# A hybrid decoder layer on one core: a reordered start, head halves in alternation, and two small moves at the ends of the MLP

## The chip, the cores and the metric

The kernel runs on one core of a Trainium2 chip. The metric is the device time of one execution in microseconds (us), median over runs. Engines are called as in the profile: PE is TensorE (PEld its weight loads), DVE VectorE, ACT ScalarE, POOL GpSimd, SP the engine that issues most DMAs. "L92" is line 92 of the kernel before.

## The reference

One decoder layer, batch 1, 256 tokens, width 2048, all in float32:

```python
h = rmsnorm(x, norm_mix_pre)
xr, yr, q, k, v, g_rnn, g_attn = split(h @ w_in)
y_rnn = rg_lru(causal_conv(xr)) * gelu(yr)
y_att = sliding_window_sink_attention(rope(q), rope(k), v, sinks)   # 32 heads, 4 key/value heads of 64
mix = sigmoid(g_rnn) * (y_rnn @ w_rnn_proj) + sigmoid(g_attn) * (y_att @ w_attn_proj)
x = x + rmsnorm(mix @ w_out, norm_mix_post)
h = rmsnorm(x, norm_mlp_pre)
u = square(relu(h @ w_mlp_up))                                       # 8192 wide
x = x + rmsnorm(u @ w_mlp_down, norm_mlp_post)
```

## The kernel before

Every large product is made from split operands: a float32 value is stored as a rounded high part and the low part that is left, and a product is the sum of high x high, high x low and low x high, three matmul passes. Weights stream from HBM in halves of 128 x 1024 (512 KB). For each, ACT writes the high part (`whi`, L91) and DVE subtracts it for the low part (`wlo`, L92). There are six buffers of each, and `Stream.ahead` keeps the splitting six halves ahead of the products.

The program is written in Python order. A scheduler then orders each engine's instructions by priority (the order of writing) and by when its own model takes the inputs to be ready. `pin` (`keep_in_program_order`) fixes an instruction behind the one written before it on its engine, `issue_after` fixes an order of issue without a wait, and `high_priority(n)` moves a block ahead by n places.

The start: the 256 tokens are two blocks of 128 (`tb`). Their x is loaded in quarters of 512 columns, ACT squares each quarter (`square`), `rms` gives the factor, DVE multiplies by factor and gain (`scale`, L349), PE transposes (`turn`, L355), and ACT and DVE store the high and low part of the transposed quarter (`part`, L361 and L362) in `hT`. The gain is spread to 128 partitions by PE: a tile of zeros with the gain in row 0, multiplied by ones (`gain_b`, L339). Between these steps stand the first k/v products (`kv_step`, which calls `b_step`, L251 to L255) for the first weight halves. The order is written out by hand, and nearly all of it is pinned. `warm` (L333) are matmuls without use for the result, issued while x is on its way.

Attention runs as a generator for each group g of key heads, one piece of it at a time between other matmuls (`pump`). The scores (`sc`, L527) take 64 rows of PE: heads of `par` 0 lie on partitions 0 to 63, those of `par` 1 on 64 to 127. The PSUM pool `psm` has two banks, which scores, transposes (`pt`) and outputs (`po`) share. For the first token block (w = 128) one bank holds four heads; for the second (w = 256) it holds two.

The MLP: `a_pair` makes a pair of 128-wide blocks of the up projection in one of two PSUM pairs (`ps`); ACT copies one half out and DVE adds the other (L240, L241). `down` begins by taking both pairs for itself (`s`), with four other banks. It forms seven of its sixteen steps by a seven-product scheme, whose sums `early` picks up; the other products and `finish` follow. At the very end (f = 1, n = 1) `finish` adds the last sums (L1033), squares them (L1037), multiplies by the gain (L1038), takes the norm and writes the output. The first half of the columns (`acc`) is multiplied by the gain in `early` (L1026).

Of the kernel before, what the change touches and what calls it, by code (L numbers as in the profile page):

```python
# [16 lines left out]
F32 = mybir.dt.float32  # L17
# [3 lines left out]
ALU = mybir.AluOpType  # L21
AX = mybir.AxisListType

P = 128
D = 2048
S = 256
TB = 2
# [24 lines left out]
class Stream:  # L52
# [35 lines left out]
    def two_parts(self, src, j):  # L88
        hi = self.pool.tile([P, 1024], F32R, tag="whi", bufs=WHALF, name=f"whi{j}")
        lo = self.pool.tile([P, 1024], F32R, tag="wlo", bufs=WHALF, name=f"wlo{j}")  # L90
        self.pin(self.nc.scalar.copy(hi, src))  # L91
        self.pin(self.nc.vector.tensor_tensor(lo, src, hi.bitcast(F32), ALU.subtract))  # L92
        return hi, lo

    def split_sums(self, j):
# [54 lines left out]
def layer(tc, x, pos_t, pos_row, inv_freq, vecs, sinks, gains, w_kv, w_q, w_xy, w_rg, w_g, w_rp, w_ap, w_out,  # L150
# [52 lines left out]
    def bank(pool, name):  # L203
        return pool.tile([P, 512], F32, tag=pool.name, name=name)
# [19 lines left out]
    def a_pair(acts, out):  # L224


        ps = pair("ps")
        for f in range(2):
            both = ps[:, f].rearrange("p a b -> p (a b)")
            for half in range(2):  # L230
                hi, lo = ws.half()
                act = [acts[kt // 4][:, kt % 4] for kt in range(half * 8, half * 8 + 8)]
                for k, a in enumerate(act):
                    mm(both, hi[:, k * P : k * P + P], a.rearrange("p a b -> p (a b)"),  # L234
                       start=half == 0 and k == 0, stop=False)
# [4 lines left out]
        nc.scalar.copy(out, ps[:, :, 1, :])  # L240
        nc.vector.tensor_tensor(out, ps[:, :, 0, :], out, ALU.add)  # L241

    def b_step(banks, acts, kt, hi, lo, last, tbs=(0, 1)):

# [47 lines left out]

    x_nat = [flat(unit(f"x{tb}", F32)) for tb in range(TB)]
    x_v = x.rearrange("(t p) d -> t p d", p=P)
    gain = flat(unit("gain", F32))
    nc.vector.memset(gain, 0.0)
    nc.scalar.dma_start(gain[0:1, :], gains[0:1])

    def quarter(q):
        return slice(q * 512, q * 512 + 512)  # L300

    for q in range(4):
        last = nc.sync.dma_start(x_nat[0][:, quarter(q)], x_v[0][:, quarter(q)])
    with tc.issue_after(last.ins):
        ws.load_to(2)
        for q in range(4):
            last = nc.sync.dma_start(x_nat[1][:, quarter(q)], x_v[1][:, quarter(q)])
# [4 lines left out]
    eps = const.tile([P, 1], F32, name="eps")  # L312
    nc.vector.memset(eps, EPS)
    st = const.tile([P, 32], F32, name="st")
    sq = const.tile([P, 4, TB, 4], F32, name="sqs")
    ones = const.tile([P, P], F32, name="ones")
    nc.vector.memset(ones, 1.0)
    make_identity(nc, ident)
    nc.scalar.activation(st[:, 31:32], eps, AF.Sqrt)

# [23 lines left out]
    def square(tb, q):  # L344
        pin(nc.scalar.activation(t2("j"), x_nat[tb][:, quarter(q)], AF.Square, accum_out=sq[:, 0, tb, q : q + 1]))

    def scale(tb, q, r):
        c = quarter(q)
        pin(nc.vector.scalar_tensor_tensor(x_nat[tb][:, c], x_nat[tb][:, c], r, gain_b[q], ALU.mult, ALU.mult))  # L349
# [13 lines left out]

    kv = [[bank(psb, f"kv{tb}")] for tb in range(TB)]

    def kv_step(j, hi, lo, tbs):
        for i in range(2):
            c = slice(i * 512, i * 512 + 512)
            b_step(kv, hT, 2 * j + i, hi[:, c], lo[:, c], 2 * j + i == KT - 1, tbs)

    for q in range(4):
        square(0, q)
    r = rms(0, 0)
    scale(0, 0, r)
    scale(0, 1, r)
    turn(0, 0)
    ws.split_to(1)
    square(1, 0)
    part(0, 0)
    turn(0, 1)  # L380
    square(1, 1)
    scale(0, 2, r)
    ws.split_to(2)
    held = [ws.half(False) for j in range(2)]
    square(1, 2)
    part(0, 1)
    turn(0, 2)
    square(1, 3)
    scale(0, 3, r)
    kv_step(0, *held[0], (0,))  # L390
    part(0, 2)
    turn(0, 3)
    r = rms(1, 0)
    scale(1, 0, r)
    part(0, 3)
    kv_step(1, *held[1], (0,))
    turn(1, 0)
    scale(1, 1, r)
    part(1, 0)
    turn(1, 1)  # L400
    ws.split_to(3)
    scale(1, 2, r)
    part(1, 1)
    turn(1, 2)
    kv_step(0, *held[0], (1,))
    ws.split_to(4)
    scale(1, 3, r)
    part(1, 2)
    turn(1, 3)
    part(1, 3)  # L410
    kv_step(1, *held[1], (1,))
    for j in range(2, 8):
        if j == 4:
            ws.pin = lambda i: i
        kv_step(j, *ws.half(), (0, 1))

    pos_i = pa.tile([P, TB], I32, name="pos_i")
    nc.sync.dma_start(pos_i, pos_t)
    ifr = pa.tile([P, 32], F32, name="ifr")
    nc.sync.dma_start(ifr, inv_freq.partition_broadcast(P))  # L420
    sink = pa.tile([P, NH], F32, name="sink")
    nc.sync.dma_start(sink, sinks.partition_broadcast(P))
    vec = pa.tile([P, 8, KT], F32, name="vec")
    nc.sync.dma_start(vec, vecs.rearrange("p (a b) -> p a b", a=8))


    mask1 = pa.tile([P, S], F32, name="mask1")
# [68 lines left out]
    def attention(g, banks):  # L496
# [11 lines left out]
        for tb in range(TB):  # L508
# [9 lines left out]
            stat = pa.tile([P, 4, 8], F32, tag="stat", bufs=3, name="stat")  # L518
            sk = sink[:, 8 * g : 8 * g + 8]
            tiles = []  # L520
            for par in range(2):
                r0 = par * HD
                for j in range(4 // per):
                    ps = bank(psm, "sc")
                    for i in range(per):
                        h = j * per + i
                        mm(ps[:, i * w : i * w + w], qT[r0 : r0 + HD, h, tb * P : tb * P + P],  # L527
                           kT[r0 : r0 + HD, g, 0:w], start=True, stop=True)
# [25 lines left out]
            for par in range(2):  # L554
                for kb in range(nk):
                    ps = bank(psm, "pt")
                    for h in range(4):
                        s3, at = tiles[par * (4 // per) + h // per]
# [413 lines left out]
    for f in range(2):  # L972
# [39 lines left out]
        def early(ready):  # L1012
# [6 lines left out]
            for i in range(2):  # L1019
                g = wpool.tile([P, 1024], F32, tag="wraw", bufs=WRAW, name=f"g3{i}")  # L1020
                nc.sync.dma_start(g, gains[3][i * 1024 : i * 1024 + 1024].partition_broadcast(P))
                g3.append(g)
            for tb in range(TB):
                for i in range(2):
                    c = quarter(i)
                    nc.vector.tensor_tensor(acc[tb][:, c], acc[tb][:, c], g3[0][:, c], ALU.mult)  # L1026

        def finish(name, b, t):
            tb, i = name
# [8 lines left out]
            nc.vector.tensor_tensor(t, a, g3[1][:, quarter(i)], ALU.mult)  # L1038
# [89 lines left out]
```

## Time and profile before

| | |
|---|---|
| median of 3 runs | 1552.69 us (1552.5 to 1554.2) |
| the profiled execution | 1553.58 us, span 1551.8 us |
| mean granted PE clock | 0.993 |
| PE busy | 1525.7 us (98%) |
| DVE, ACT, POOL busy | 1117.5, 843.9, 1.7 us |
| read from HBM | 288.60 MB, 190 GB/s over the span |

The span runs from the first to the last instruction; the profiled execution's own time is 1.78 us longer. In a row of the timeline stand the start and the length of a run of equal instructions, the engine (a q behind it: its sequencer), the line, what is written from what, the shapes, the count, and in brackets the idle time of the engine before it with what ended it. A row of the waits gives who waited for whom, the total, the number of times and the longest. A row of the windows gives the stretch, its length, then busy time and count of PE, PEld, DVE, ACT and POOL, the granted PE clock, the DMA engines' share and GB/s. Matmuls overlap their neighbours in these rows, so the pace of PE is read from start to start.

### The profile page before, as it was taken

The numbers are of one execution on the slowest core, as the hardware profiler recorded it, in microseconds if no ns is written. First come the engines' busy times: TensorE is split into PE (matmuls) and PEld (weight loads), VectorE is DVE, ScalarE is ACT, GpSimd is POOL, SyncE is SP. The second block draws the span as 40 slices with busy tenths as digits, with TensorE's granted clock in tenths as the row PEclk, the third lists the DMA queues.
The fourth block names the chain that finished last, engine by engine and source line by source line (L and its number), as shares of the span: only waits on it lengthen the run. The fifth ranks groups of instructions, "written<-read, shape, count | busy, mean of one in ns | idle before, by whom it ended". The sixth has DMA issues, their size and how long they took to land.

```text
span 1551.8 us, 20974 instructions
## 1 busy us (share of the span) xinstructions
PE 1525.7 (98%) x8042; PEld 1295.5 (83%) x8042; DVE 1117.5 (72%) x1364; ACT 843.9 (54%) x1156; POOL 1.7 (0%) x9
## 2 busy tenths in 40 slices
PE   8999999999999999999999999999999999999997
PEld 6887777888888888888787888888888888888885
DVE  6666666866859877555655866688886666788997
ACT  5555545646647766444344655555454555555553
POOL 0000000000000000000000000000000000000000
PEclk9999999999999999999999999999999999999999
DMA  6554354354655465555663855556666655566664
GB/s 246 188 169 148 115 173 147 124 191 149 229 188 177 158 213 198 190 184 190 250 221 98 278 190 189 187 175 213 218 203 218 221 187 189 188 242 232 203 216 138
DMA packets 82902, 296.26 MB, mean 191 GB/s; under 512 B 9585, under 2 KB 9841, under 8 KB 81777
## 3 DMA queue, kind: packets, MB, share of 16 engines
q1 hardware_dynamic: 79344, 285.48, 55.7%
q10 hardware_dynamic: 3458, 9.45, 1.6%
q8 instruction: 63, 1.03, 0.3%
q14 instruction: 37, 0.30, 0.1%
HBM read 288.60 MB, written 6.29 MB: 190 GB/s over the span
## 4 chain that ended last, share of the span: by engine, by line
PE 87%; DVE 5%; ACT 3%; DMA 3%; issue 2%; SPq 0%; DVEq 0%; ACTq 0%
PE ps L234 36%; PE ps L237 18%; PE dQ L908 7%; PE s L908 4%; PE dP L908 3%; DVE wlo L92 2%; PE dCs L908 2%; DMA wraw<-in_w_dn 2%; PE o L251 2%; PE o L255 2%; PE o L253 2%; PE q L251 2%; PE q L253 2%; PE q L255 2%; PE sc L527 1%
## 5 line engine op out<-in xcount | busy, mean ns | idle before, releaser
L92 DVE TENSOR_TENSOR wlo<-wraw,whi 128x1024 fp32r<-128x1024 f32 x528 | 639.8, 1221 | 322.4 <-ACT whi L91 317.0
L91 ACT CAST whi<-wraw 128x1024 fp32r<-128x1024 f32 x528 | 549.0, 1049 | 585.9 <-PE ps L234 271.5
L234 PE MATMUL ps<-hT,whi 128*128 128x512 f32 x1024 | 260.5, 394 | 0.0
L234 PE MATMUL ps<-h2T,whi 128*128 128x512 f32 x1024 | 258.2, 394 | 0.5 <-DVE h2T L280 0.5
L234 PEld LDWEIGHTS ps<-hT,whi 128*128 128x128 f32 x1024 | 183.8, 189 | 36.5 <-issue 3.5
L234 PEld LDWEIGHTS ps<-h2T,whi 128*128 128x128 f32 x1024 | 185.3, 190 | 34.2 <-DVE h2T L280 0.9
L237 PEld LDWEIGHTS ps<-hT,wlo 128*128 128x128 f32 x1024 | 140.1, 190 | 11.7 <-issue 2.0
L237 PEld LDWEIGHTS ps<-h2T,wlo 128*128 128x128 f32 x1024 | 140.0, 191 | 10.1
L237 PE MATMUL ps<-hT,wlo 128*128 128x256 f32 x1024 | 145.3, 283 | 0.0
L237 PE MATMUL ps<-h2T,wlo 128*128 128x256 f32 x1024 | 143.0, 283 | 0.0
L908 PE MATMUL dQ<-whi,uT 128*128 128x512 f32 x288 | 106.5, 389 | 0.0
L234 PE MATMUL ps<-yrnn,whi 128*128 128x512 f32 x256 | 64.4, 393 | 0.7 <-DVE yrnn L700 0.7
L234 PE MATMUL ps<-yatt,whi 128*128 128x512 f32 x256 | 64.1, 392 | 0.0
L908 PEld LDWEIGHTS dQ<-whi,uT 128*128 128x128 f32 x288 | 54.1, 188 | 11.2
L908 PE MATMUL dQ<-wlo,uT 128*128 128x512 f32 x144 | 56.1, 390 | 1.6 <-DVE wlo L92 1.6
L111 DVE TENSOR_TENSOR tlo<-t,thi 128x1536 fp32r<-128x1536 f32 x28 | 49.2, 1757 | 10.1 <-ACT thi L110 10.1
L908 PE MATMUL dP<-whi,uT 128*128 128x512 f32 x144 | 53.8, 389 | 0.0
L908 PE MATMUL dCs<-whi,uT 128*128 128x512 f32 x144 | 53.7, 389 | 0.0
L234 PEld LDWEIGHTS ps<-yrnn,whi 128*128 128x128 f32 x256 | 46.0, 189 | 9.3 <-DVE yrnn L700 1.1
L234 PEld LDWEIGHTS ps<-yatt,whi 128*128 128x128 f32 x256 | 46.0, 189 | 8.2
L251 PE MATMUL q<-whi,hT 128*128 128x512 f32 x128 | 51.1, 399 | 0.0
L253 PE MATMUL q<-wlo,hT 128*128 128x512 f32 x128 | 50.2, 392 | 0.0
(251 smaller groups left out, 2068.6 us busy)
## 6 DMA issues: line engine op xcount, KB each, us to landing
wraw<-in_w_up SPq DMA_DIRECT2D x128, 512.0 KB, 4.6
wraw<-in_w_dn SPq DMA_DIRECT2D x128, 512.0 KB, 4.5
wraw<-in_w_g SPq DMA_DIRECT2D x64, 512.0 KB, 4.4
wraw<-in_w_xy SPq DMA_DIRECT2D x64, 512.0 KB, 3.9
wraw<-in_w_q SPq DMA_DIRECT2D x32, 512.0 KB, 4.3
wraw<-in_w_ap SPq DMA_DIRECT2D x32, 512.0 KB, 3.8
wraw<-in_w_rp SPq DMA_DIRECT2D x32, 512.0 KB, 4.6
wraw<-in_w_out SPq DMA_DIRECT2D x32, 512.0 KB, 4.8
```

What stands on the lines that cost most here:

```text
L91: self.pin(self.nc.scalar.copy(hi, src))
L92: self.pin(self.nc.vector.tensor_tensor(lo, src, hi.bitcast(F32), ALU.subtract))
L111: v.tensor_tensor(lo, t, hi.bitcast(F32), ALU.subtract)
L234: mm(both, hi[:, k * P : k * P + P], a.rearrange("p a b -> p (a b)"), start=half == 0 and k == 0, stop=False)
L237: mm(ps[:, f, 1, :], lo[:, k * P : k * P + P], a[:, 0, :], start=False, stop=half == 1 and k == 7)
L251: mm(banks[tb][n], a[:, 0, t], hi[:, n * 512 : n * 512 + 512], start=first, stop=False)
L253: mm(banks[tb][n], a[:, 0, t], lo[:, n * 512 : n * 512 + 512], start=False, stop=False)
L255: mm(banks[tb][n], a[:, 1, t], hi[:, n * 512 : n * 512 + 512], start=False, stop=last)
L527: mm(ps[:, i * w : i * w + w], qT[r0 : r0 + HD, h, tb * P : tb * P + P], kT[r0 : r0 + HD, g, 0:w], start=True, stop=True)
L908: mm(b, a[x], w[y], start=not begun and i == 0, stop=tail and i == 2)
```

## The change

Four things are changed.

*The start.* `eps` and `ones` are set first; the gain's tile is cleared in quarters, three by DVE and one by POOL. x is loaded in two halves a block. The odd quarters are squared by DVE (`square_v`). Three scalings of the first block come ahead of the first weight splits. The low parts of the first four weight halves are subtracted on POOL (`ws.low = nc.gpsimd`). The k/v products are split into those with the high and those with the low weights (`kv_part`) and placed anew, and the halves from the third to the sixth are split at written places (`split`). Four small loads (`pos_i`, `ifr`, `sink`, `vec`) are queued behind x.

*Attention.* The loops over `par` and over the heads change places, with two banks taken at once.

*The last up pair.* For p = 15, in both f, the copy and the addition at the end of `a_pair` have a higher priority (300).

*The finish.* The four multiplications of `acc` by the gain go from `early` to `finish`, two for each token block.

```diff
@@ Stream @@
+        self.low = nc.vector
...
-        self.pin(self.nc.vector.tensor_tensor(lo, src, hi.bitcast(F32), ALU.subtract))
+        self.pin(self.low.tensor_tensor(lo, src, hi.bitcast(F32), ALU.subtract))
@@ a_pair @@
-        nc.scalar.copy(out, ps[:, :, 1, :])
-        nc.vector.tensor_tensor(out, ps[:, :, 0, :], out, ALU.add)
+        with tc.high_priority(prio) if prio else ExitStack():
+            nc.scalar.copy(out, ps[:, :, 1, :])
+            nc.vector.tensor_tensor(out, ps[:, :, 0, :], out, ALU.add)
@@ the loads @@
-    nc.vector.memset(gain, 0.0)
-    nc.scalar.dma_start(gain[0:1, :], gains[0:1])
...
+    for q in range(4):
+        (nc.gpsimd if q == 3 else nc.vector).memset(gain[:, quarter(q)], 0.0)
+    nc.scalar.dma_start(gain[0:1, :], gains[0:1])
+
+    def load_x(tb):
+        for c in (slice(0, 1024), slice(1024, 2048)):
+            last = nc.sync.dma_start(x_nat[tb][:, c], x_v[tb][:, c])
+        return last
@@ the first norm @@
+    def square_v(tb, q):
+        c = quarter(q)
+        pin(nc.vector.scalar_tensor_tensor(t2("j"), x_nat[tb][:, c], 1.0, x_nat[tb][:, c], ALU.mult, ALU.mult,
+                                           accum_out=sq[:, 0, tb, q : q + 1]))
...
+    def kv_part(j, tb, low):
+        for i in range(2):
+            kt = 2 * j + i
+            c = slice(i * 512, i * 512 + 512)
+            a, t = hT[kt // 4][:, kt % 4], slice(tb * P, tb * P + P)
+            hi, lo = held[j]
+            if low:
+                mm(kv[tb][0], a[:, 0, t], lo[:, c], start=False, stop=kt == KT - 1)
+            else:
+                mm(kv[tb][0], a[:, 0, t], hi[:, c], start=kt == 0, stop=False)
+                mm(kv[tb][0], a[:, 1, t], hi[:, c], start=False, stop=False)
...
+    square(0, 0)
+    square_v(0, 1)
+    square(0, 2)
+    square_v(0, 3)
+    r = rms(0, 0)
+    ws.low = nc.gpsimd
+    scale(0, 0, r)
+    turn(0, 0)
+    scale(0, 1, r)
+    turn(0, 1)
+    scale(0, 2, r)
+    part(0, 0)
+    split(1)
+    part(0, 1)
+    split(2)
+    kv_part(0, 0, False)
+    turn(0, 2)
+    scale(0, 3, r)
+    square(1, 0)
+    square_v(1, 1)
+    square(1, 2)
+    square_v(1, 3)
+    kv_part(1, 0, False)
+    turn(0, 3)
+    kv_part(0, 0, True)
+    r = rms(1, 0)
+    scale(1, 0, r)
+    part(0, 2)
+    turn(1, 0)
+    split(3)
+    scale(1, 1, r)
+    part(0, 3)
+    kv_part(1, 0, True)
+    turn(1, 1)
+    kv_part(2, 0, False)
+    part(1, 0)
+    split(4)
+    part(1, 1)
+    kv_all(0, 1)
...
+    ws.low = nc.vector
...
+    with tc.issue_after(last.ins):
+        nc.sync.dma_start(pos_i, pos_t)
...
@@ attention @@
-            for par in range(2):
-                r0 = par * HD
-                for j in range(4 // per):
-                    ps = bank(psm, "sc")
-                    for i in range(per):
-                        h = j * per + i
-                        mm(ps[:, i * w : i * w + w], qT[r0 : r0 + HD, h, tb * P : tb * P + P],
+            for j in range(4 // per):
+                both = [bank(psm, "sc") for par in range(2)]
+                for i in range(per):
+                    h = j * per + i
+                    for par in range(2):
+                        r0 = par * HD
+                        mm(both[par][:, i * w : i * w + w], qT[r0 : r0 + HD, h, tb * P : tb * P + P],
                            kT[r0 : r0 + HD, g, 0:w], start=True, stop=True)
+                for par in range(2):
+                    ps = both[par]
@@ the up projection @@
-            a_pair(h2T, wide(u))
+            a_pair(h2T, wide(u), PRIO if p == PAIRS - 1 else 0)
@@ early @@
-            for tb in range(TB):
-                for i in range(2):
-                    c = quarter(i)
-                    nc.vector.tensor_tensor(acc[tb][:, c], acc[tb][:, c], g3[0][:, c], ALU.mult)
@@ finish @@
             if i == 0:
+                for k in range(2):
+                    c = quarter(k)
+                    nc.vector.tensor_tensor(acc[tb][:, c], acc[tb][:, c], g3[0][:, c], ALU.mult)
                 return
```

More of the change, by code (lines that the diff above doesn't have):

```diff
@@ L222, in pair, with a_pair @@
         return pool.tile([P, 2, 2, S], F32, tag="pair" + pool.name, name=name)
-    def a_pair(acts, out):
+    def a_pair(acts, out, prio=0):
         ps = pair("ps")
@@ L294, in layer @@
     x_v = x.rearrange("(t p) d -> t p d", p=P)
-    gain = flat(unit("gain", F32))
-    nc.vector.memset(gain, 0.0)
-    nc.scalar.dma_start(gain[0:1, :], gains[0:1])
     def quarter(q):
         return slice(q * 512, q * 512 + 512)
-    for q in range(4):
-        last = nc.sync.dma_start(x_nat[0][:, quarter(q)], x_v[0][:, quarter(q)])
-    with tc.issue_after(last.ins):
+    eps = const.tile([P, 1], F32, name="eps")
+    nc.vector.memset(eps, EPS)
+    ones = const.tile([P, P], F32, name="ones")
+    nc.vector.memset(ones, 1.0)
+    gain = flat(unit("gain", F32))
+    for q in range(4):
+        (nc.gpsimd if q == 3 else nc.vector).memset(gain[:, quarter(q)], 0.0)
[4 more added lines that the diff above has]
+        return last
+    with tc.issue_after(load_x(0).ins):
         ws.load_to(2)
-        for q in range(4):
-            last = nc.sync.dma_start(x_nat[1][:, quarter(q)], x_v[1][:, quarter(q)])
+        last = load_x(1)
     with tc.issue_after(last.ins):
@@ L373, in layer, with kv_all, split @@
+    def kv_all(j, tb):
+        kv_part(j, tb, False)
+        kv_part(j, tb, True)
+    held = []
+    def split(n):
+        ws.split_to(n)
+        while len(held) < n:
+            held.append(ws.half(False))
+    square(0, 0)
+    square_v(0, 1)
+    square(0, 2)
+    square_v(0, 3)
     r = rms(0, 0)
+    ws.low = nc.gpsimd
     scale(0, 0, r)
+    turn(0, 0)
     scale(0, 1, r)
-    turn(0, 0)
-    ws.split_to(1)
-    square(1, 0)
[L379 to L382, printed above, removed]
@@ L407, in layer @@
+    kv_all(1, 1)
+    ws.low = nc.vector
+    part(1, 2)
     scale(1, 3, r)
-    part(1, 2)
     turn(1, 3)
+    split(5)
+    kv_part(3, 0, True)
     part(1, 3)
-    kv_step(1, *held[1], (1,))
-    for j in range(2, 8):
+    kv_all(2, 1)
+    kv_all(3, 1)
+    split(6)
+    for j in range(4, 8):
         if j == 4:
             ws.pin = lambda i: i
-        kv_step(j, *ws.half(), (0, 1))
+        if j > 5:
+            held.append(ws.half())
+        for tb in range(TB):
+            kv_all(j, tb)
@@ L557, in attention @@
                     for h in range(4):
-                        s3, at = tiles[par * (4 // per) + h // per]
+                        s3, at = tiles[h // per * 2 + par]
                         nc.tensor.transpose(ps[:, h * P : h * P + P], s3[:, h % per, kb * P : kb * P + P], ident)
```

33 lines of the change are left out of this document (5 added, 28 removed).

## The prediction

> **What bounds the kernel now.** I read the page's totals first, then the waits of TensorE, then the timeline of each stretch that the change touches.
>
> ```profile
> span 1551.8 us, 20974 instructions
> PE 1525.7 (98%) x8042; PEld 1295.5 (83%) x8042; DVE 1117.5 (72%) x1364; ACT 843.9 (54%) x1156; POOL 1.7 (0%) x9
> PE 87%; DVE 5%; ACT 3%; DMA 3%; issue 2%; SPq 0%; DVEq 0%; ACTq 0%
> ```
> ```profile
> PE ptr L355 <- DVE x L349: 2.0, 1, 2.0
> PE s L908 <- DVE u L241: 1.9, 2, 1.1
> PE dQ L908 <- DVE wlo L92: 1.6, 1, 1.6
> PE kv L251 <- ACT hT L361: 1.5, 2, 0.9
> ```
> TensorE (PE) is busy for 98% of the span and makes 87% of the chain that ended last. Whatever shortens its work, or ends one of its few waits, shortens the run; work of VectorE (DVE), ScalarE (ACT) or the DMAs counts only where a PE wait hangs on it. The edits reach four places: the scores of attention, the two waits on `u L241`, the wait on `wlo L92` near the end, and the first 43 us.
>
> **Part 1, head halves in turn.** The scores use 64 of the 128 rows: even heads rows 0-63, odd heads rows 64-127. Before, all of one half come first; now the halves alternate, each with a PSUM bank of its own.
>
> ```profile
> 6.83 3.73 PE L339 MATMUL gain_b<-gain,ones 128*128 128x512 f32 x8 [0.28 <-DMA gain<-in_gains]
> 100.43 1.71 PE L527 MATMUL sc<-kT,qT 64*128 64x128 f32 x16
> 102.07 2.12 PE L234 MATMUL ps<-hT,whi 128*128 128x512 f32 x8
> 114.44 1.13 PE L527 MATMUL sc<-kT,qT 64*128 64x256 f32 x4
> 115.50 0.73 PE L234 MATMUL ps<-hT,whi 128*128 128x512 f32 x2
> 116.27 1.13 PE L527 MATMUL sc<-kT,qT 64*128 64x256 f32 x4
> 118.35 1.99 PE L527 MATMUL sc<-kT,qT 64*128 64x256 f32 x8
> 120.27 0.50 PE L251 MATMUL q<-whi,hT 128*128 128x512 f32 x1
> 138.94 1.94 PE L567 MATMUL po<-pT,v_sb 128*64 128x512 f32 x8
> 140.81 0.50 PE L251 MATMUL q<-whi,hT 128*128 128x512 f32 x1
> 100.76 0.72 PE L527 MATMUL sc<-kT,qT 64*128 64x128 f32 x7
> ```
> Does alternating buy anything? Two rows say so. Eight f32 passes of 512 columns that use the whole array (`gain_b`) take 3.73 us; the eight of `po`, which alternate between two halves of the columns, take 140.81-138.94 = 1.87. And rows pair as columns do: from 4 to 8 passes of 256 columns the row grows by 1.99-1.13 = 0.86, so 0.215 a pass and 0.108 for 128 columns; yet in the last row, where the first half's passes of a 16-pass group hand over to the second's, seven 128-column passes take 0.72, which is under 7 x 0.108 before any start or drain.
>
> A group of 8 passes lasts 120.27-118.35 = 1.92 = 8 x 0.215 + 0.20. In pairs: 4 x 0.215 + 0.20 = 1.06, so 0.86 saved; one such group for each of four key groups g: 3.4 us. The group of 16 lasts 102.07-100.43 = 1.64; eight slots of 0.108 and 0.20 make 1.06; with four of them 2.3, and I take 2.2. The two groups of 4 I leave at nothing: they stand apart by 1.8 us with other matmuls between, because the second bank comes free only then (`po` holds it); the first bank's two heads will still go alone. Should they pair, each g saves another 1.06: 4.2. If nothing pairs, 0. **Part 1: 5.6 (0 to 9.8).** Nothing else is late behind it: ACT and DVE split weights six halves ahead, and PE has no wait on them in this stretch.
>
> **Part 2, last up pair.** `down` needs both PSUM pairs that the up projection used, so its first `s` products wait until the last pair is copied out.
>
> ```profile
> 1030.60 1.49 ACT L110 CAST thi<-t 128x1536 fp32r<-128x1536 f32 x1 [2.54 <-DVE t L107]
> 1031.98 1.04 ACT L91 CAST whi<-wraw 128x1024 fp32r<-128x1024 f32 x1
> 1032.93 0.58 ACT L240 COPY u<-ps 128x512 f32<-128x512 f32 x1
> 1034.20 0.68 DVE L241 TENSOR_TENSOR u<-ps,u 128x512 f32<-128x512 f32 x1
> 1034.94 0.50 PE L908 MATMUL s<-thi,seven 128*128 128x512 f32 x1 [0.79 <-DVE u L241]
> 1379.68 0.50 PE L908 MATMUL s<-thi,seven 128*128 128x512 f32 x1 [1.12 <-DVE u L241]
> ```
> The copy waited behind a `whi` cast (1.04), and the addition behind a `wlo` subtraction. Moved ahead of one of each they end over 1 us sooner, and PE needs 0.79 and 1.12. The casts that step back serve weights several steps later. **Part 2: 1.9 (0.8 to 1.9).**
>
> **Part 3, last scaling at the finish.** Before, four multiplications by the gain stand in `early`, ahead of the last weight split:
>
> ```profile
> 1526.27 0.68 DVE L1026 TENSOR_TENSOR acc<-acc,g 128x512 f32<-128x512 f32 x1
> 1531.07 1.89 DVE L1026 TENSOR_TENSOR acc<-acc,g 128x512 f32<-128x512 f32 x3
> 1532.88 1.22 DVE L92 TENSOR_TENSOR wlo<-wraw,whi 128x1024 fp32r<-128x1024 f32 x1
> 1534.15 0.50 PE L908 MATMUL dQ<-wlo,uT 128*128 128x512 f32 x1 [1.62 <-DVE wlo L92]
> 1540.68 0.68 DVE L1033 TENSOR_TENSOR acc<-dP,t 128x512 f32<-128x512 f32 x1
> 1541.40 0.69 DVE L1038 TENSOR_TENSOR t<-acc,g 128x512 f32<-128x512 f32 x1
> 1543.09 0.69 DVE L1033 TENSOR_TENSOR acc<-dQ,t 128x512 f32<-128x512 f32 x1 [1.00 <-PE dQ L908]
> ```
> Without them (0.60 from start to start) the split comes 4 x 0.60 = 2.4 earlier and the 1.62 wait goes. They come back in `finish`: two with the first token block, two between 1541.40 and 1543.09. There DVE is idle for only 1.00, and PE's last product now comes 1.62 earlier, so up to 1.2 of queue could meet it; the first block's work, however, also starts earlier. **Part 3: 1.3 (0.4 to 1.6).**
>
> **Part 4, the start.** It is reordered wholesale and I am least sure of it.
>
> ```profile
> 6.42 0.63 ACT L345 ACTIVATE j<-x 128x512 f32<-128x512 f32 x1
> 10.12 0.63 ACT L345 ACTIVATE j<-x 128x512 f32<-128x512 f32 x1 [2.98 <-DMA x<-in_x]
> 11.66 1.41 DVE L349 SCALAR_TENSOR_TENSOR x<-x,st,gain_b 128x512 f32<-128x512 f32 x2
> 12.98 1.22 DVE L92 TENSOR_TENSOR wlo<-wraw,whi 128x1024 fp32r<-128x1024 f32 x1
> 43.30 1.07 PE L234 MATMUL ps<-hT,whi 128*128 128x512 f32 x4
> 13.75:20.58 6.83, 5.97 (x18) 4.52 (x18) 5.81 (x10) 4.87 (x13) 0.00 (x0) 0.50 1.03 412
> 0.74 0.38 SPq L418 DMA_DIRECT2D pos_i<-in_pos_t  x1
> 43.01 0.16 DVE L441 CAST posf<-pos_i 128x2 f32<-128x2 int32 x1
> 1.47 0.40 POOL L430 TENSOR_SCALAR_AFFINE_SELECT mask<-mask 128x256 f32<-128x256 f32 x1
> ```
> The first scaling starts at R = 11.66, the k/v products end at 43.30: 31.6 us. The PE work in it is 96 products (16 k tiles, 2 token blocks, 3 passes) at 0.227 (1.07 for four is about that plus a drain) and 32 transposes at about 0.11: 25.3. So 6.3 us are lost, part of it in the stretch from 13.75 to 20.58, whose granted clock was 0.50.
>
> *R.* The last quarter of x comes at 10.12 though the third was there by 6.42. Now `pos_i` leaves the head of SP's queue (0.38 of issue) and x comes in two loads a block. That gives 0.4 at least and 3.7 at most; I take 1.0. The squares halve between ACT and DVE, but only one (0.63) followed the last arrival anyway. The gain's memset in pieces, `eps` and `ones` ahead of it, and the small loads behind x lie beside this wait; their first user stands at 43.01.
>
> *After R.* DVE scales three quarters back to back; the first four `wlo` go to GpSimd (POOL). ACT alternates halves of hT and `whi`. Adding up DVE at 0.67 a scaling or subtraction and ACT at 0.58 and 1.05, the second block's first transposed part is there at R+11.2, by which time PE has 7.2 us of its work done; the remaining 18.1 end at R+29.3 if nothing else is late: 2.3 better than 31.6. New waits: PE's `kv` low products wait for POOL's `wlo`, and the transposes of the second block are pinned behind them. A POOL subtraction is in no row. From below it is DVE's 1.22; from above, a one-input select takes 0.40 for 256 columns, so 1.6 for 1024 and 3.2 for two inputs. I take the middle, 2.2: the first starts when its `whi` is there, R+3.4, and the first two end at R+5.6 and R+7.8, before the transposes behind them have their bank (R+9.1).
>
> The `square_v` of the second block fall at R+5.3, inside those subtractions. Should each stand still until POOL's instruction ends, up to 2.2 us each, the second norm slips by about 2.5 and the end goes to R+32: part 4 would give 0.6 in place of 3.3. [...]
>
> The other risk is the clock. PE has longer idle gaps between R+2 and R+9 now; if a second stretch of 6.83 us is granted 0.50, up to 3.4 us more are lost. I take R+30.6, a gain of 1.0, and 1.0 for R. **Part 4: 2.0 (-2.5 to 4.5).**
>
> **Sum.** 5.6 + 1.9 + 1.3 + 2.0 = 10.8 us. The profiled execution took 1553.58 (its span and 1.78 around it), 0.89 over the median of the three runs, 1552.69. Less 10.8: 1542.8 for that execution, 1541.9 for the median.
>
> **The rivals.**
> *The start gives back what it gains* (both mechanisms of part 4 at once, -2.5): 8.8 - 2.5 = 6.3, so 1546.4. For it: the overlap with `square_v` and the 0.50 stretch. Against it: PE has 6.3 us of loss there already to be eaten first.
> *Halves don't pair* (PE's order keeps the passes of a half together, or the second bank comes late everywhere): 5.2 left, 1547.5. Against it: the sevenfold row.
> *Everything pairs and the start runs through*: 9.8 + 1.9 + 1.6 + 4.5 = 17.8, so 1534.9.
> *Slower: POOL is the bound of the start.* Four subtractions of T each follow one another from R+3.4; PE has about 11.8 us of k/v work behind the last (48 products of the last four halves and the fourth's low ones). The stage then ends at R+15.2+4T, with R 1.0 earlier: 4T-17.4 lost against 31.6. Parts 1 to 3 give 8.8, so it shows as slower from T = 7.4, six times DVE's 1.22; at T = 8 the time is 1558.5. Against it: the select rows, 3.2 at most.
>
> **How the numbers follow.** About 0.2% (3.1 us) is what a measurement of this kernel can tell from no change. Chances: the forecast 0.50, start given back 0.18, no pairing 0.08, everything 0.10, POOL the bound 0.07; 0.07 are left for an order of the scheduler that I can't see, spread from 1546 to 1556. The range 1534.5 to 1549.5 leaves out POOL as the bound, about half of that rest, and the ends of the parts coinciding. Faster 0.87, same 0.05, slower 0.08.
>
> **What would show it.** Scores: the 16-pass groups at about 1.1 us and the late 8-pass ones at 1.06, the early ones still split in 4 and 4 with 1.06 each. No PE wait on `u L241`; none on `wlo L92` after 1500. The first `ps L234` at about 41 in place of 43.30; a POOL row `wlo` of about 2.2 us; DVE's squares of the second block stretched beyond 0.75 if POOL blocks them. Wrong would be: an 8-pass group still at 1.9, POOL rows over 4 us, or new PE waits in the middle of the run where none were.

## The result and the profile after

The changed kernel takes 1556.54 us (median of 20 runs, 1553.61 to 1559.70), the kernel before 1552.79 (20 runs beside it): ratio 1.0022, 95% interval 1.0014 to 1.0030. It is slower by about 3.5 us where 10.8 us of gain were forecast; that way out had been given a chance of 0.08, nearly all of it with POOL as the bound.

The profiled execution hides this: with 1553.61 us it is the fastest of the 20, and its span equals that of before. The page's totals:

```profile
span 1551.8 us, 20965 instructions
PE 1520.3 (98%) x8042; PEld 1288.1 (83%) x8042; DVE 1119.6 (72%) x1370; ACT 842.6 (54%) x1148; POOL 12.1 (1%) x14
PE 83%; DVE 7%; ACT 4%; DMA 4%; issue 2%; POOL 0%; DVEq 0%; ACTq 0%; POOLq 0%
```
PE's share of the chain that ended last fell from 87 to 83%, and DVE's, ACT's and DMA's rose. The waits of PE say where:

```profile
PE dQ L956 <- DVE wlo L93: 4.0, 2, 3.6
PE gain_b L344 <- DMA gain<-in_gains: 3.5, 1, 3.5
PE ptr L365 <- DVE hT L372: 2.0, 1, 2.0
PE kv L384 <- DMA wraw<-in_w_g: 1.7, 1, 1.7
PE pt L607 <- DVE s L598: 1.4, 4, 0.5
PE dQ L956 <- ACT whi L92: 0.8, 1, 0.8
```
The wait on the last `wlo`, which was to vanish, grew from 1.6 to 3.6 us (4.0 with a second one). At the start stands a wait on the gain's row. The 1.7 us that the list puts down to `wraw` is a wait for POOL's second low part, which ended at 20.56, just ahead of the product; in e1 below the same wait is named so. Attention has four small waits on DVE that before did not have. The waits on `u` are gone from the list.

Three stretches in which PE had work were granted half the clock (columns as in the windows view shown of before; the granted clock is the third number from the end):

```profile
8.27:11.69 3.42, 3.42 (x5) 1.35 (x4) 0.26 (x1) 0.00 (x0) 0.00 (x0) 0.50 1.03 420
21.90:28.75 6.85, 5.41 (x17) 4.53 (x18) 4.37 (x8) 3.83 (x6) 4.75 (x2) 0.50 0.72 270
1530.60:1534.00 3.40, 3.40 (x8) 2.63 (x9) 2.94 (x5) 0.72 (x2) 0.00 (x0) 0.50 0.02 5
```
Each costs PE at most half its length, here 6.8 us together: within the first a `gain_b` pass takes 0.85 us from start to start, behind it 0.43. (The kernel before lost up to 3.4 us in the same way in its start, from 13.75 to 20.58.) They follow idle time of PE: the gap of 3.51 us ahead of `gain_b`; gaps of 1.18 and 1.71 us between 14 and 21 us and one of 1.99 us, in which the second stretch begins; the gap of 3.62 us in which PE waits for the last `wlo`. How much idle time draws a stretch is not shown: the one at 751 us in the kernel before stands behind a gap of only 2.09 us.

Whether a given gap draws a stretch differs from one profiled execution to the next. The one of before had stretches of 3.4 us at 751 and of 6.8 us at 846, behind gaps which the changed kernel has too (2.09 us at 748, 0.83 and 1.21 us ahead of 845), and where its own profiled execution drew none. Near the end, e8 (below) drew one behind 1.74 us and e4 none behind 2.43. The two stretches of before make up to 5.1 us, enough for two profiles to show equal spans where the medians differ by 3.5 us. So below, medians say how much, and stages of a profile say where.

**The start**, in the timeline:

```profile
2.75 0.52 ACTq L307 DMA_DIRECT2D gain<-in_gains  x1
...
7.40 0.16 DVE L332 RECIPROCAL st<-st 128x1 f32<-128x1 f32 x1 [0.36 <-ACT st L331]
7.95 5.37 PE L344 MATMUL gain_b<-gain,ones 128*128 128x512 f32 x8 [3.51 <-DMA gain<-in_gains]
11.43 1.41 DVE L359 SCALAR_TENSOR_TENSOR x<-x,st,gain_b 128x512 f32<-128x512 f32 x2 [3.87 <-PE gain_b L344]
15.40 5.16 POOL L93 TENSOR_TENSOR wlo<-wraw,whi 128x1024 fp32r<-128x1024 f32 x2 [12.60 <-ACT whi L92]
17.10 1.25 DVE L354 SCALAR_TENSOR_TENSOR j<-x 128x512 f32<-128x512 f32 x1
18.29 2.82 DVE L354 SCALAR_TENSOR_TENSOR j<-x 128x512 f32<-128x512 f32 x1
23.20 2.38 POOL L93 TENSOR_TENSOR wlo<-wraw,whi 128x1024 fp32r<-128x1024 f32 x1 [2.64 <-ACT whi L92]
46.88 1.98 PE L235 MATMUL ps<-hT,whi 128*128 128x512 f32 x8
```
The norm's factor is there at 7.40 (before, the last square alone started at 10.12), but the first scaling still starts at 11.43 (11.66 before): it waits for the first half of `gain_b`, whose row was issued at 2.75 and came in 5.2 us later, with the larger loads on their way; and `gain_b` then ran at half clock for 3.4 of its 5.37 us (3.73 before). The k/v stage ends at 46.88 in place of 43.30. From the first scaling to that end it takes 35.4 us, 31.6 before: so the larger part of the loss arises behind the first scaling. There PE waits 1.7 us for POOL and 2.0 us for DVE, whose queue was held up by the squares of the second norm (1.25 and 2.82 us beside POOL, 0.69 without it), and then goes through 6.85 us at half clock.

**The scores** and the last `po` of attention:

```profile
104.09 1.16 PE L573 MATMUL sc<-kT,qT 64*128 64x128 f32 x16
119.63 1.13 PE L573 MATMUL sc<-kT,qT 64*128 64x256 f32 x4
122.04 1.14 PE L573 MATMUL sc<-kT,qT 64*128 64x256 f32 x8
124.24 1.13 PE L573 MATMUL sc<-kT,qT 64*128 64x256 f32 x4
312.50 1.94 PE L615 MATMUL po<-pT,v_sb 128*64 128x512 f32 x8
```
The group of 16 takes 105.18 - 104.09 = 1.09 by the start of the next row (1.64 before), a group of 8 takes 123.11 - 122.04 = 1.07 (1.92 before). So heads pair as worked out.

**The end**:

```profile
1453.13 0.39 PE L956 MATMUL s<-whi,seven 128*128 128x512 f32 x1
1524.42 0.69 DVE L1087 TENSOR_TENSOR acc<-acc,g 128x512 f32<-128x512 f32 x1 [1.34 <-DMA g<-in_gains]
1529.22 1.22 DVE L93 TENSOR_TENSOR wlo<-wraw,whi 128x1024 fp32r<-128x1024 f32 x1
1530.50 0.72 PE L956 MATMUL dQ<-wlo,uT 128*128 128x512 f32 x1 [3.62 <-DVE wlo L93]
1542.47 0.39 PE L956 MATMUL dQ<-whi,uT 128*128 128x512 f32 x1
```
and the same two ends of the last `down` in the kernel before:

```profile
1458.70 0.39 PE L908 MATMUL s<-whi,seven 128*128 128x512 f32 x1
1542.67 0.39 PE L908 MATMUL dQ<-whi,uT 128*128 128x512 f32 x1
```
From the first `s` product to the end of the last product it takes 1543.06 - 1458.70 = 84.4 us before and 1542.86 - 1453.13 = 89.7 after. PE came to it 5.6 us earlier and left it at the same time; up to 5.1 of the 5.6 are the stretches that the changed kernel's execution did not draw.

### The profile page after: what moved, and what is told of

It reads as the page before. It is cut to its first block, busy times and chain, and to the rows that moved or that the text cites. A ratio compares the mean times of both kernels' runs of the same rounds, so it can differ in the third digit from the quotient of the medians.

```text
span 1551.8 us, 20965 instructions
## 1 busy us (share of the span) xinstructions
PE 1520.3 (98%) x8042; PEld 1288.1 (83%) x8042; DVE 1119.6 (72%) x1370; ACT 842.6 (54%) x1148; POOL 12.1 (1%) x14
## 4 chain that ended last, share of the span: by engine, by line
PE 83%; DVE 7%; ACT 4%; DMA 4%; issue 2%; POOL 0%; DVEq 0%; ACTq 0%; POOLq 0%
PE ps L235 35%; PE ps L238 18%; PE dQ L956 5%; PE s L956 3%; DVE wlo L93 3%; DMA wraw<-in_w_dn 3%; PE dP L956 3%; PE dCs L956 2%; PE o L253 2%; PE o L255 2%; PE o L257 2%; PE q L253 2%; PE q L255 2%; PE q L257 2%; ACT whi L92 2%
```

## Experiments

In the table the "stage" is the end of the k/v stage (start of the first `ps` row), the "last down" is measured as above, and "stretch" is what was granted half clock within it; these three are from one profiled execution each. Ratios are to the kernel before on the same chip, and rows can come from different chips; 0.001 is 1.55 us.

| kernel | ratio (95%) | stage | last down | stretch |
|---|---|---|---|---|
| before | 1 | 43.3 | 84.4 | 0 |
| changed | 1.0022 (1.0014-1.0030) | 46.9 | 89.7 | 3.4 |
| e1_start | 1.0035 (1.0022-1.0049) | 47.9 | 89.7 | 6.8 |
| e2_scores | 0.9974 (0.9960-0.9988) | 42.1 | 84.4 | 0 |
| e3_pair | 1.0017 (1.0003-1.0030) | 42.0 | 90.0 | 3.4 |
| e4_finish | 1.0001 (0.9985-1.0016) | 43.3 | 85.2 | 0 |
| e5_squares | 1.0028 (1.0015-1.0040) | 45.1 | 88.2 | 3.4 |
| e6_gain | 1.0010 (0.9998-1.0022) | 40.2 | 90.0 | 6.8 |
| e7_last | 1.0010 (0.9999-1.0021) | 48.2 | 91.2 | 6.8 |
| e8_combo | 0.9989 (0.9976-1.0003) | 42.2 | 89.0 | 3.4 |
| e9_end | 0.9983 (0.9970-0.9997) | 43.0 | 82.4 | 0 |
| e10_scores_end | 0.9954 (0.9938-0.9970) | 42.7 | 82.4 | 0 |
| e11_all | 0.9955 (0.9939-0.9971) | 39.3 | 83.0 | 0 |
| e12_nopair | 0.9961 (0.9947-0.9975) | 42.2 | 82.4 | 0 |
| e13_change_end | 0.9992 (0.9982-1.0002) | 47.1 | 84.1 | 0 |
| e14_pair_end | 0.9957 (0.9942-0.9972) | 42.6 | 85.2 | 0 |
| e15_change_gain | 0.9996 (0.9983-1.0009) | 44.8 | 91.3 | 6.8 |

The stage scatters, in part with the clock: the eight kernels that have the old start end it between 42.0 and 43.3, the four with the new start as it is between 46.9 and 48.2.

**The four parts alone.** Each of e1 to e4 is the kernel before with one of the four diffs shown above.

> The kernel before with the new start alone. Parts theory (each part acts for itself): slower by about 3.6 us, which is how much later the first ps product starts in the changed kernel's profile (46.88 against 43.30); the gain_b products again wait some 3.5 us for the gain's DMA, and DVE's squares of the second block again take 1.2 and 2.8 us. End theory (the split chain of the last weights sets the end, so that what PE wins or loses earlier is partly swallowed by its wait there): the start is 3.6 us later as well, but the wait of 1.62 us on the last wlo shrinks to nothing, so only about 2 us are left.

> The kernel before with the alternating head halves alone. Parts theory: faster by about 3.4 us (the stretch from the first ps product to the last po took 266.97 in place of 270.37), and the wait on the last wlo stays near 1.6. End theory: PE reaches the down projection 3.4 us sooner, and the wait on the last wlo grows to 3 to 5 us, so that the time is lower by 0 to 1.5 us only.

> The kernel before with the higher priority of the last up pair alone. Parts theory: faster by about 1.9 us, the two waits on u are gone. End theory: the waits are gone, but the wait on the last wlo grows from 1.6 to about 3.5, and the time stays within 0.5 us of before.

> The kernel before with the last scaling moved to the finish alone. Order theory (the move itself changes the order at the end for the worse): slower by 2 to 4 us, with one scaling standing ahead of the early sums and waiting for the gain's DMA, and a PE wait of 3 us or more on the last wlo. End theory: the wait on the last wlo stays at about 1.6 or shrinks, and the time is lower by 0 to 1.6 us.

Measured: +0.35%, -0.26%, +0.17%, +0.01%, in sum +0.27% or 4.2 us; the whole change has 3.4. The parts add up within the intervals. Neither theory holds for all: the scores keep their gain to the end, while the pair, whose waits on `u` are gone in e3's trace too, loses. Those waits were no fixed cost, however: among the kernels without the priority PE waits on `u` for 1.9 us in before, 1.4 in e6, 0.8 in e1, 0.6 in e2 and e4, 0.4 in e5, while in e9, e10 and e12 no such wait is listed:

```profile
PE s L910 <- DVE u L241: 0.6, 2, 0.4
```
is the row of e2. With the priority 0 to 0.5 us are left. In e3 PE waits at the end for

```profile
PE dQ L909 <- DVE wlo L92: 4.1, 2, 3.4
```
and in e4, where the scalings were to make room for the last split, for

```profile
PE dQ L908 <- DVE wlo L92: 2.4, 1, 2.4
```
That is more than the 1.6 of before. In e4's timeline one moved scaling stays ahead of the last `wlo` even so, and so do the sums of `early`, between these two rows:

```profile
1523.30 0.68 DVE L1039 TENSOR_TENSOR acc<-acc,g 128x512 f32<-128x512 f32 x1
...
1528.10 1.22 DVE L92 TENSOR_TENSOR wlo<-wraw,whi 128x1024 fp32r<-128x1024 f32 x1
```
Counted from the first `s` product (at 1454.93 here), that `wlo` starts 73.2 us into the last `down`, 74.2 before: 1.0 us earlier and not 2.4. PE in turn stops for it at 72.0 us, 73.8 before, because its products were ordered anew. So the wait is longer.

**The start: POOL or the gain?** e5 is the start alone with the second block's squares on ACT; e6 the start alone with

```diff
     gain = flat(unit("gain", F32))
-    for q in range(4):
-        (nc.gpsimd if q == 3 else nc.vector).memset(gain[:, quarter(q)], 0.0)
     nc.scalar.dma_start(gain[0:1, :], gains[0:1])
...
-        mm(gain_b[q], ones, gain[:, quarter(q)], start=True, stop=True)
+        mm(gain_b[q], ones[0:1, :], gain[0:1, quarter(q)], start=True, stop=True)
```

> The new start alone, but all four squares of the second token block on ACT (two of them leave DVE, which no longer has an instruction with two SBUF inputs beside POOL's subtractions). Port theory (POOL's low subtractions hold up DVE's squares, 0.69 -> 1.25 and 2.82 us, and with them the second norm): the second norm comes about 2 us earlier, the k/v stage ends near 46 in place of 47.9, the time stands at +4 to +4.5 against the kernel before (the start alone had +6.3). Gain theory (the late gain row and the slow gain_b set the stage): ACT has 2 x 0.63 more to do and nothing is won, +6 to +7.

> The new start alone, but the gain is loaded as one row at the head of ACT's queue and spread by products with one row of ones (K = 1), so that no clearing of a tile stands ahead of it. Gain theory: the row lands about 2 us earlier or more, gain_b is done by 8 to 10, the first scaling starts near 8 to 10 in place of 11.4 to 11.6, the k/v stage ends 2 to 3.5 us earlier and the time stands at +3 to +4. Port theory: the first scaling comes earlier, but POOL's four subtractions and the held-up second norm stand where they stood, less than 1 us is won, +5.5 to +6.3.

Measured: 1.0028 and 1.0010 where the start alone has 1.0035. In e6 the row is issued at the head of ACT's queue, and

```profile
4.22 4.06 PE L341 MATMUL gain_b<-gain,ones 1*128 1x512 f32 x8
7.63 2.06 DVE L356 SCALAR_TENSOR_TENSOR x<-x,st,gain_b 128x512 f32<-128x512 f32 x3
40.23 1.07 PE L235 MATMUL ps<-hT,whi 128*128 128x512 f32 x4
```
the first scaling comes at 7.63 and the stage ends 7.6 us earlier than in e1. Part of the 7.6 is the clock: from `gain_b` on, e1's start has 12.0 us at half clock (last section) and e6's 6.8, which makes up to 2.6 us. The gain theory holds, and by more than expected in the stage; 3.9 us (0.25%) are seen in the time. Where the rest goes is not shown: the last `down` is as long in both (89.7 and 90.0), and in the profiles e6 loses up to 5.1 us to the stretches near 748 and 844, which e1 did not draw. In e5, DVE's second norm comes at

```profile
20.61 0.16 DVE L331 RECIPROCAL st<-st 128x1 f32<-128x1 f32 x1 [0.36 <-ACT st L330]
```
in place of 22.50 in e1, and the stage ends 2.8 us earlier than in e1. But e5's start has 7.9 us at half clock against e1's 12.0, so up to 2.0 of the 2.8 can be the clock's. The intervals of e1 and e5 overlap too. So the squares' hold-up is seen in the norm; its part of the time (about 1 us) is not shown.

**The end.** e7 is the changed kernel, e8 the kernel before with scores, pair and finish, both with the last splits at a higher priority:

```diff
-        parts = [[ws.half(False) for i in range(2)] for p in range(held)]
+        with tc.high_priority(PRIO) if held == 3 else ExitStack():
+            parts = [[ws.half(False) for i in range(2)] for p in range(held)]
```

> The changed kernel with a higher priority (300) for the splits of the last three steps of the last down, so that the last wlo no longer stands behind nine 0.6 us sums. End theory (the last wlo, behind the sums, sets when PE goes on, and the wait of 3.6 us brings a stretch at half clock): the wait falls from 3.6 to about 1.5 or less, the half-clock stretch near 1531 goes or gets rarer, the time is 2 to 5 us below the changed kernel (1556.5): 1551.5 to 1554.5. Landing theory (the last weight's landing sets it, the order of DVE does not matter): within 1 us of the changed kernel.

> Scores, last up pair and finish as in the changed kernel, the start as before, and the higher priority for the last splits. End theory (the pair's 1.9 us were won and then lost at the end): -3.8 of the scores, -1.9 of the pair and 1 to 3 at the end: 1544 to 1546.5 with the kernel before at 1553. Rival (the pair's loss has another cause than the last split): -3.8 + 2.0 and 1 at the end: 1549 to 1551.

e7 stands 1.9 us (0.12%) under the changed kernel, with overlapping intervals, at the edge of what the end theory wanted; but the signs that this theory named failed: PE's wait fell only from 3.6 to 2.5 us, and the last `down` drew 6.8 us at half clock. e8 misses it as well: 1.7 us (0.11%) gained is even less than its rival gave. The order of DVE alone isn't enough: in e8 ACT stands idle ahead of three of the last high parts, waiting for the weights to land:

```profile
1518.48 1.06 ACT L91 CAST whi<-wraw 128x1024 fp32r<-128x1024 f32 x1 [1.61 <-DMA wraw<-in_w_dn]
1521.08 1.05 ACT L91 CAST whi<-wraw 128x1024 fp32r<-128x1024 f32 x1 [1.54 <-DMA wraw<-in_w_dn]
1523.63 1.04 ACT L91 CAST whi<-wraw 128x1024 fp32r<-128x1024 f32 x1 [1.50 <-DMA wraw<-in_w_dn]
```
A load is issued only once an earlier split has freed one of the program's four raw buffers (between 1450 and 1545 us of the kernel before, SP's queue waits for a `wlo` 21 times, 40.2 us in all), so a late split makes the next landing late. Therefore e9 to e12 also load the last chunk into a free tile, and hold the moved scalings behind the addition of their block:

```diff
-            if j < 2 * EXTRA:
+            if j < 2 * EXTRA or j >= 2 * len(self.chunks) - 2:
                 if j % 2 == 0:
                     self.place = self.room(f"wraw{j}")
...
-            nc.vector.tensor_tensor(a, b, t, ALU.add)
+            add = nc.vector.tensor_tensor(a, b, t, ALU.add)
...
+                with tc.issue_after(add.ins):
                     for k in range(2):
```
e9 is the kernel before with this end alone, e10 adds the scores; e11 is the changed kernel with this end, the gain row of e6 and the squares of e5; e12 is e11 without the pair's priority.

> The kernel before with only its end changed: the last two weight halves are loaded into a free tile of their own (so they need not wait for a raw buffer), the last splits have the higher priority, and the four scalings go to the finish, each behind the addition of its block. End theory: the last wlo is ready about 5 us earlier, PE's wait of 1.6 us goes and with it the half-clock stretches that longer waits there bring: the time falls by 1.5 to 4 us, the last down takes 82 to 83 us (84.4 before). Pace theory (the landings of all loads in the last down set the pace of the splits, the last one's place does not matter): within 0.7 us, PE waits as long on an earlier wlo.

> Head halves in turn and the same new end, the start and the up pairs as before. If both act: -3.8 and -1.5 to -4: 5.3 to 7.8 us below the kernel before. If the end gives nothing: -3 to -4.

> The changed kernel with the three repairs: gain row loaded at the head of ACT's queue and spread with K = 1, the second block's squares on ACT, and the new end. Gain and port theory: the k/v stage ends at 38 to 39.5 (46.9 in the changed kernel, 40.2 with the gain row alone); end theory: no wait over 1 us near the end. Together 8 to 12 us below the changed kernel, 5 to 8 us below the kernel before. If the end keeps what the start gives (the last down lengthens again to 89 to 90 us): 3 us below the kernel before or less.

> As the one before this, but the last up pair without its priority. If the priority only brings forward the down (its 1.9 us kept once the end is repaired): 1 to 2 us slower than the one before this. If it costs elsewhere (+2.0 alone): 1 to 3 us faster than the one before this.

e9 gives 0.9983, 2.6 us. In its trace no PE wait is left in the last `down`, and its two ends are

```profile
1456.06 0.39 PE L908 MATMUL s<-whi,seven 128*128 128x512 f32 x1
1538.12 0.39 PE L908 MATMUL dQ<-whi,uT 128*128 128x512 f32 x1
```
that is 82.4 us: the 1.6 us wait of before and little else. The end theory holds. With the scores it comes to 0.9954 (7.1 us), the sum of the two. e11 and e12 are within the interval of e10, and not told apart from each other: over the old start, the new one with its repairs shows no further gain, though in e11 its stage ends at 39.3. In e12 it ended at 42.2; there PE ran at half pace for the first 19 us, as described in the last section.

**How much is the start's, how much the end's?** e13 is the changed kernel with only the end of e9; e14 is e10 with the pair's priority; e15 is the changed kernel with only e6's gain row.

> The changed kernel with only its end repaired (the last two halves loaded into a tile of their own, the last splits ahead, the moved scalings behind the additions). End theory: the last down takes 82 to 83.5 us in place of 89.7, no half-clock stretch there, and 5 to 7 us come back: 1549.5 to 1551.5 by the changed kernel's median of 1556.5, so 1 to 3 us below the kernel before; its difference to the next one is the start's own price, 4 to 6 us. If the start's loss was only brought out by the end: the difference to the next one is under 2 us.

> Head halves in turn, the last up pair's priority and the repaired end, with the start of before. If the pair's 1.9 us are kept once the end is repaired: 1 to 2 us faster than the same without the priority (0.9954 of the kernel before), 0.994 to 0.9948. If the priority costs in itself: 0.996 or more.

> The changed kernel with only the gain's row loaded first and spread with K = 1. Gain theory: the k/v stage ends near 40 in place of 46.9; by the median 4 to 5 us come back (1556.5 to 1552), as with the start alone, where 5.1 did, and the last down still takes 88 to 91 us. If the end takes it back: under 2 us.

e13: 0.9992, so 4.7 us (0.30%) of the changed kernel's time were lost at the end. By e9 the kernel before loses 2.6 us there too, so the change itself added about 2. e13 against e14: 0.35%, 5.4 us, is the start's own price with the end repaired. e15: 0.9996, 4.0 us of that price hang on the gain's row alone, and the last `down` still takes 91.3. e14 against e10 (0.9957 and 0.9954): the medians show neither gain nor loss of the pair's priority where the end is repaired. The difference is uncertain by some 0.2% to each side, so neither 1.9 us of gain nor e3's loss of 2.6 is excluded. The traces say more. e10 has no PE wait in its last `down`; e14, which differs from it only by the priority, has

```profile
PE dQ L911 <- DVE wlo L92: 1.9, 3, 1.1
```
and takes 85.2 us for it in place of 82.4: its splits lag.

What lengthens the last `down` in e1, e5 and e6 is only partly settled. From the first product of the MLP on, PE, DVE and ACT run the same instructions in the same order in these three as in the kernel before (3504 on PE, 597 on DVE, 434 on ACT). DVE waits longer for weights to land in the last `down`, however; the rows of before, of e1 and of the changed kernel, over its first 62 us or so:

```profile
DVE t L104 <- DMA wraw<-in_w_dn: 0.2, 1, 0.2
```
```profile
DVE t L105 <- DMA wraw<-in_w_dn: 3.1, 5, 1.0
```
```profile
DVE t L105 <- DMA wraw<-in_w_dn: 3.9, 6, 1.1
```
Loads there take from 3.5 to 6.0 us from issue to landing. Where some come late, every later split comes later, since the next load waits for the split; PE's wait grows from 1.6 to between 3.3 and 3.5 us, and behind it stands in these three runs a half-clock stretch worth up to 1.7 or 3.4 us. In the twelve kernels with the new start or the pair's priority these DVE waits make 1.0 to 4.5 us, in the other five 0.2 to 1.4. Why is open; one profile of each can't tell a cause from chance. That the end need not hang on them is shown by e11 and e12: they have 2.6 and 2.0 us of these waits, and their last `down` takes 83.0 and 82.4.

## Why the prediction was wrong

The forecast was 14 us off, and by the runs about half of that is the start's.

**Part 4, the start (forecast 2.0 gained, measured 0.35% or 5.4 us lost; by the stage 3.6 lost).** Both terms failed. *R* was to come 1.0 earlier and came 0.2 earlier. It took the last quarter of x as the gate and put the gain's memset "beside this wait". x did come as early as the most hopeful bound had it, but the gain's row, which had landed at 6.83 before, landed at 7.95. With it at 6.83 and `gain_b` at full pace, its first half would have been ready near 8.6 (an estimate: four passes at 0.43 us, the pace without the stretch). The late row cost 1.1 us of that, the half clock on four passes 1.7. e6 shows the forecast's R to be reachable, and passed, with the row first.

The larger miss is *After R*: 30.6 us were taken and 35.4 measured. The part had named both mechanisms that did it, one with R+32 and one with 3.4 us more, which makes R+35.4, and then took R+30.6, as if they would hardly come. Both came. DVE's squares were stretched to 1.25 and 2.82 us, and the second half-clock stretch took 6.85 us. POOL's subtractions took 2.37 to 2.81 us where 2.2 was taken, and the second result was there at R+9.1 in place of R+7.8. That the sum comes out so exactly is in part luck: the slow second half of `gain_b` also kept PE from its first transposes until R+1.7. In e6, with the squares beside POOL and 6.8 us of half clock too, but the gain early, the stage takes 32.6 us behind the first scaling.

The squares and POOL held each other up: both squares ended 0.55 us behind a subtraction (at 18.36 and 21.11, behind 17.81 and 20.57), and the subtraction between them took 2.81 us, in e5 without those squares 2.36. The three others took 2.37 to 2.41. The forecast had the hold-up as a supposition, since no row of before has a subtraction on POOL; these rows show it, 1.25 and 2.82 us for squares that take 0.69 without POOL.

**Part 3, the finish (forecast 1.3 gained, measured 0).** "Without them (0.60 from start to start) the split comes 4 x 0.60 = 2.4 earlier and the 1.62 wait goes" failed twice. The scheduler put one of the four still ahead of the last `wlo`, in the changed kernel even with 1.34 us of waiting for the gain's load `g`. And the last split stands behind the sums and behind the `wlo` before it, which waits for its weight to land (in the changed kernel 1.55 us for the `whi`, and that 1.72 us for the load), and not behind the scalings alone: it came 1.0 us earlier in e4, PE came 1.8 us earlier, and waited longer.

**Part 2, the last up pair (forecast 1.9 gained, alone 0.17% or 2.6 us lost).** Two steps failed. The 1.9 us of waits on `u` were taken from one execution; the nine kernels without the priority show 0 to 1.9, seven of them under 1, so there was less to gain. And "The casts that step back serve weights several steps later" held them to be free: in e3 PE waits 4.3 us on `wlo` in the last `down` (4.1 of it behind 1500 us, as shown; 1.6 before), in e14 1.9 us where e10 has none. In e3 a half-clock stretch came on top. How much of e3's 2.6 us is the priority's and how much the end's is not shown.

**Part 1, the scores (forecast 5.6, measured 0.26% or 4.0 us).** The mechanism and every size of a group were right: 4 x (1.64 - 1.09) + 4 x (1.92 - 1.07) = 5.6. The time alone, with its interval of 1.9 to 6.2 us, would not contradict it. What was too large is the term for the stage: from the first `ps` row to the last `po` it is 312.50 - 46.88 = 265.6 against 312.32 - 43.30 = 269.0 before, so 3.4 saved; e2 gives 3.5. "Nothing else is late behind it" failed: PE's transposes now wait for the softmax, four times and 1.4 us in all (`pt <- DVE s`, also in e2, where no such wait stood before). The last 0.8 us are open.

**The risk that had no place in the sum** was that of the end: the forecast let the run end with PE's work shortened. The last `down` was bound by a chain of buffer, load and split whose 1.62 us of wait it had quoted. That row was read as the cost of four scalings, when it was the first sign of another bound; the change lost about 2 us more there than the kernel before. A slower run had been tied to POOL alone, with subtractions from 7.4 us on; they took 2.8 at most. It came from the gain's row, the squares and the clock at the start, and from the splits at the end.

## What to carry to other kernels

Where an input is made to come earlier, list what else its first user waits for, and find in the trace when each of these is there: the next one late sets the gain. Price a risk that a row already shows: the 0.50 stretch stood in the trace before. Take a small wait from more than one execution before its whole length is counted as gain. Where PE is busy all the time but for a few waits, look at the last stretch: if the chain of buffer, load and split that feeds it is not ahead, time saved earlier can be waited out there (it was for the pair, it was not for the scores). A wait behind which the clock drops cost half as much again or more here: 3.3 to 3.6 us of wait, and up to 1.7 or 3.4 for the stretch. The version to choose is e10: head halves in turn and the repaired end, 0.9954 of the kernel before; e11 and e12 are no faster and change more.

## What the runs showed of the hardware

A row of 8 KB that was issued at 2.75 us, with 2 MB of bulk loads issued from 0.74 on, landed after 5.2 us (PE's wait for it ended at 7.95); issued at 0.73 in e6, it was there by 4.22.

Two f32 score products that use different halves of PE's rows start 6 or 7 ns apart (128 columns) or 13 to 14 ns apart (256 columns) in the changed kernel, and the next two follow after 0.11 or 0.22 us.

PE's start was slower than the granted clock in the windows view tells. In e12 and e15 `gain_b`, the same eight passes as in e6 (4.06 us) and started at nearly the same time, took

```profile
4.37 7.19 PE L342 MATMUL gain_b<-gain,ones 1*128 1x512 f32 x8
```
or 0.85 us from pass to pass, as `gain_b` had in the half-clock stretch of the changed kernel. The view of e15 gives the clock as 1.00 there. But the clock's records in that trace begin only at 19.0 us, in e12's at 19.1, and where there is no record the view shows 1.00. In e12, around that time:

```profile
17.81 0.63 PE L384 MATMUL kv<-whi,hT 128*128 128x512 f32 x1
18.23 0.63 PE L385 MATMUL kv<-whi,hT 128*128 128x512 f32 x1
21.18 0.40 PE L384 MATMUL kv<-whi,hT 128*128 128x512 f32 x1
21.41 0.40 PE L385 MATMUL kv<-whi,hT 128*128 128x512 f32 x1
```
0.42 us from start to start ahead of the first record, 0.23 behind it. In the seven traces that have such passes ahead of the first record (e1, e4, e5, e7, e8, e12, e15) PE keeps the pace of half clock there, 0.85 us a pass for `gain_b` and 0.43 for the k/v products, and has 0.43 and 0.23 behind it. That record comes at 4.9 us in the changed kernel, 6.9 in before, 13.0 in e1, 12.8 in e5 and 4.0 in e6. Counted from `gain_b` on, half clock thus takes 6.9 us of the start in before, 10.2 in the changed kernel, 12.0 in e1, 7.9 in e5, 6.8 in e6 and 18.0 in e15. Half of the 11.2 us between e6 and e15 is enough for the 4.6 us by which e15's stage ends later. Why the first record is so late in e12 and e15 is open.
